# First weights of a second block split during the last expert pair, and a choice of experts by small look-ups: a two-block transformer on one core

## The chip, the core and the metric

The kernel runs on one core of a Trainium2 chip. A core has five engines that run side by side, each with its own queue of instructions, issued in order: TensorE (PE: matrix products; its weight loads are shown as PEld), VectorE (DVE), ScalarE (ACT), GpSimd (POOL) and SyncE (SP), which here mostly issues the DMA loads of the weights. The metric is device time in microseconds (us) from start to end of the program. Three runs of the kernel before took 1753.63, 1758.73 and 1759.56 us; the median is 1758.73 us.

## The reference

Two transformer blocks follow each other on 256 tokens of width 1024, all in float32.

```python
def first_block(x, ...):
    h = x + mixed @ w_out            # stick-breaking attention and spatial gating
    h = h + hierarchical_moe(rmsnorm(h), ...)   # 4 groups x 8 experts, top 2 of a group
    return rmsnorm(h, final_norm_g)

def second_block(x, mem, ...):
    u = rms_norm(h, norm_mix)
    qa, ka, va, qb, kvb, gb, gate_a, gate_b = split(u @ w_in)   # differential and sparse attention
    h = h + merged @ w_out
    h = h + memory_cross_attention(...)
    h = h + peer_ffn(rms_norm(h, norm_ffn), ...)
    return rms_norm(h, norm_final)

def peer_ffn(u, w_q, sub_keys, u_tab, v_tab):     # 16384 experts, tables of 16384 x 1024
    s = einsum(q(u), sub_keys)                    # 8 heads x 2 halves x 128 keys for each token
    top_s, top_i = top_k(s, 16)                   # 16 of each half
    best_s, best_j = top_k(all 16 x 16 sums, 16)  # 16 pairs for each head
    expert = take_along_axis(cand_i, best_j)      # row index * 128 + column index
    g = softmax(best_s)
    out = sum_k g[k] * gelu(u . u_tab[expert[k]]) * v_tab[expert[k]]
```

## The kernel before

Float32 products are made of three products of a narrower form: each weight tile is split into a high part (a copy on ScalarE, L145) and a low part (weight minus high part, on VectorE or GpSimd, L146), and `mm3` (L153 to L155) adds high x high, high x low and low x high. Three buffers each hold high and low parts (`n_hi`, `n_lo`), so a split can start when the half tile three places before it has been used.

The first block ends with `moe`: 32 experts in 16 pairs, p = 0 to 15. A pair takes gate and up products (L777), a silu, transposes, a down product into two accumulators (L805), whose results ScalarE copies out (high part, L813) and VectorE subtracts (low part, L814), and a product by a one-hot matrix that brings the rows back to the tokens; VectorE adds these to X (L716). After `moe` come a rarely needed overflow branch and `phase_c`, the second block. `split_first` (L864 to L871) splits the first quarter of the second block's `w_in` ahead of `phase_c`: high parts L869 on ScalarE, low parts L870 on GpSimd. `phase_c` flips X (eight pairs of transposes L216, with the high part by L217 on ScalarE and the low part by L221 on VectorE; their instructions are kept in the list `flips`), then takes the products of X by the first two quarters, and scales X by its norm.

The expert layer of the second block takes all 16384 rows of U as 64 tiles of two halves (a half is one split of 128x1024 and 24 matmuls), while the choice runs beside it: top-k steps on VectorE (L1423 to L1447), candidates' positions (L1458 to L1469), the softmax (L1474 to L1481, with Exp on ScalarE, L1477), the transposes of its weights on TensorE (L1485), and the look-ups of the chosen indices. A look-up takes, for each of 256 choices a token, the entry at a position 0 to 15 of a list of 16: L1499 compares a position with 0 to 15 (128x2048), L1502 multiplies by the list, L1505 sums 16 by 16; L1507 transposes. There are four of them (two halves of the tokens, row and column). Then one-hot matrices (L1516, L1519) and products L1526 spread the weights over the experts; `N_POOL` says for how many U tiles GpSimd makes the low parts (L1562: `gp=i < N_POOL`).

The order in which instructions stand in each engine's queue comes from a scheduler that simulates a timeline on its own costs; `after(a, b)` forces a behind b. Loads of weights stand in SP's queue in the order of `queue`, each waiting for its buffer (L122).

## Time and profile before

| what | value |
|---|---|
| median of three runs | 1758.73 us |
| profiled execution, its own time | 1757.5 us |
| its span, first to last instruction | 1755.8 us |
| mean granted TensorE clock | 0.989 |
| TensorE busy | 1687.8 us, 96% |
| VectorE busy | 981.4 us, 56% |
| ScalarE busy | 680.9 us, 39% |
| GpSimd busy | 304.9 us, 17% |

The profile is of one execution. Busy time is the time in which an engine has an instruction running; a share over the whole span averages over stages with different limits, so the rows below are taken from single stretches. In a timeline row the first number is the start in us from the span's start, the second how long the instruction (or the group of `xN` equal ones) ran; what stands in brackets is how long the engine had been idle before it and which engine's instruction it had waited for. [...]

### The profile page before, as it was taken

Reading aid. Unit: us, or ns where it says so; the run is one execution under the profiler, and the core shown is the slowest. Engines: PE = TensorE matmul, PEld = TensorE weight load, DVE = VectorE, ACT = ScalarE, POOL = GpSimd, SP = SyncE. Lnnn points to the kernel's source line nnn. Section 1 sums busy time; section 2 is a strip of 40 time slices with the busy share of each in tenths; the row PEclk is TensorE's granted clock in tenths of the full one; section 3 lists DMA queues with packets and bytes.
Section 4 is the critical chain, followed back from the end, with each engine's and each line's share of the span. In section 5 each row is a group of like instructions: output and inputs, shape, how many; then the busy total and the mean of one; then the engine's idle time right before and its main releaser. Section 6 shows DMA issues by size and latency. Waiting matters only on the chain. (4 is left out here: it accounts for less than half of the span.)

```text
span 1755.8 us, 27472 instructions
## 1 busy us (share of the span) xinstructions
PE 1687.8 (96%) x11096; PEld 1330.7 (76%) x11096; DVE 981.4 (56%) x2010; ACT 680.9 (39%) x1148; POOL 304.9 (17%) x176
## 2 busy tenths in 40 slices
PE   8999999999999989999999799999999999999998
PEld 7984454444444369889899799999999978888886
DVE  5462231122222165685658989999999844444444
ACT  6551121111111145455454435444444444444444
POOL 4320000000000033223457400000000022222221
PEclk9998999999999999999999899999999999999999
DMA  9537999899999985533044343444444455565553
GB/s 380 218 112 325 366 407 382 340 398 412 421 420 421 421 333 217 202 112 121 25 145 145 121 168 127 163 168 146 153 161 145 168 192 192 192 228 192 192 193 120
DMA packets 69251, 410.02 MB, mean 234 GB/s; under 512 B 9217, under 2 KB 9857, under 8 KB 28545
## 3 DMA queue, kind: packets, MB, share of 16 engines
q1 hardware_dynamic: 67840, 406.64, 61.4%
q8 instruction: 88, 1.44, 0.3%
q10 hardware_dynamic: 1280, 1.59, 0.2%
q14 instruction: 43, 0.34, 0.1%
HBM read 406.11 MB, written 2.10 MB: 232 GB/s over the span
## 5 line engine op out<-in xcount | busy, mean ns | idle before, releaser
L145 ACT ACTIVATE hi<-w 128x1024 fp32r<-128x1024 f32 x368 | 388.9, 1059 | 506.3 <-PE oa L155 180.6
L146 DVE TENSOR_TENSOR lo<-w,hi 128x1024 fp32r<-128x1024 f32 x260 | 326.9, 1259 | 223.3 <-ACT hi L145 223.1
L146 POOL TENSOR_TENSOR lo<-w,hi 128x1024 fp32r<-128x1024 f32 x108 | 266.9, 2473 | 1011.7 <-ACT hi L145 947.0
L155 PE MATMUL acc<-act,lo 128*128 128x256 f32 x928 | 268.4, 289 | 6.0 <-DVE lo L146 6.0
L153 PE MATMUL acc<-act,hi 128*128 128x256 f32 x928 | 267.7, 289 | 4.0 <-ACT hi L145 2.8
L154 PE MATMUL acc<-act,hi 128*128 128x256 f32 x928 | 265.4, 286 | 0.0
L777 PE MATMUL acc<-w,act 128*64 128x512 f32 x1016 | 246.1, 596 | 4.7 <-DMA w<-w_up 3.5
L154 PE MATMUL acc<-lo,act 128*128 128x256 f32 (+1 forms) x592 | 196.6, 333 | 3.4 <-DVE lo L146 1.6
L155 PE MATMUL acc<-hi,act 128*128 128x256 f32 (+1 forms) x592 | 195.3, 332 | 0.2 <-DVE act L1286 0.2
L155 PEld LDWEIGHTS acc<-act,lo 128*128 128x128 f32 x928 | 179.6, 194 | 10.2 <-DVE lo L146 7.6
L153 PEld LDWEIGHTS acc<-act,hi 128*128 128x128 f32 x928 | 179.6, 194 | 9.4 <-ACT hi L145 5.5
L777 PEld LDWEIGHTS acc<-w,act 128*64 128x64 f32 x1016 | 80.4, 137 | 139.3 <-issue 126.4
L153 PE MATMUL acc<-hi,act 128*128 128x256 f32 (+1 forms) x592 | 177.3, 334 | 3.6 <-ACT hi L145 1.6
L154 PEld LDWEIGHTS acc<-act,hi 128*128 128x128 f32 x928 | 179.6, 194 | 1.2 <-issue 1.2
L153 PE MATMUL oa<-act,hi 128*128 128x256 f32 x528 | 151.7, 287 | 4.0 <-ACT hi L145 3.9
L155 PE MATMUL oa<-act,lo 128*128 128x256 f32 x528 | 152.5, 289 | 0.0
L154 PE MATMUL oa<-act,hi 128*128 128x256 f32 x528 | 150.6, 285 | 0.0
L1519 DVE SCALAR_TENSOR_TENSOR oha<-cols,iT,g 128x384 bf16<-128x384 bf16 x256 | 142.0, 609 | 0.0
L153 PEld LDWEIGHTS acc<-hi,act 128*128 128x128 f32 x592 | 113.4, 192 | 16.7 <-ACT hi L145 3.6
L154 PEld LDWEIGHTS acc<-lo,act 128*128 128x128 f32 x592 | 113.4, 192 | 16.3 <-DVE lo L146 3.3
L805 PE MATMUL oa<-w,mo_h 128*64 128x512 f32 x480 | 125.0, 599 | 0.0
L155 PEld LDWEIGHTS acc<-hi,act 128*128 128x128 f32 x592 | 113.1, 192 | 10.4 <-DVE act L1286 0.4
(423 smaller groups left out, 2523.3 us busy)
## 6 DMA issues: line engine op xcount, KB each, us to landing
w<-w_gate SPq DMA_DIRECT2D x64, 1024.0 KB, 10.7
w<-peer_u SPq DMA_DIRECT2D x64, 1024.0 KB, 4.9
w<-peer_v SPq DMA_DIRECT2D x64, 1024.0 KB, 4.9
w<-w_up SPq DMA_DIRECT2D x63, 1024.0 KB, 12.2
w<-w_down SPq DMA_DIRECT2D x60, 1024.0 KB, 10.6
w<-w_in SPq DMA_DIRECT2D x28, 1024.0 KB, 9.0
w<-w_out SPq DMA_DIRECT2D x8, 1024.0 KB, 16.0
w<-peer_wq SPq DMA_DIRECT2D x8, 1024.0 KB, 4.8
```

The source lines that it names most:

```text
L145: self.last_hi = nc.scalar.activation(hi, src, AF.Copy)
L146: r = (nc.gpsimd if gp else nc.vector).tensor_tensor(lo, src, _f(hi), op=ALU.subtract)
L153: first = mm(ps, lhsT=a[0], rhs=b[0], start=start, stop=False)
L154: mm(ps, lhsT=a[0], rhs=b[1], start=False, stop=False)
L155: return first, mm(ps, lhsT=a[1], rhs=b[0], start=False, stop=stop)
L777: mm = nc.tensor.matmul(ps[nm][e * 64:(e + 1) * 64, :], lhsT=xe[kh][:, k, s0:s0 + CAP], rhs=w[e][:, k, :], start=(kh + k == 0), stop=(kh * ...
L805: nc.tensor.matmul(y[hf][e * 64:(e + 1) * 64, :], lhsT=hT[:, kh * 2 + k, e * 64:(e + 1) * 64], rhs=w[e][k][:, hf * 512:(hf + 1) * 512], st ...
L1519: V.scalar_tensor_tensor(ab[:, t], cols[:, None, :].to_broadcast([128, 3, 128]), iT[:, t0 + t:t0 + t + 1], g3[:, :, t0 + t:t0 + t + 1].to_ ...
```

## The change

1. `N_POOL` falls from 7 to 3: the low parts of U tiles 3 to 6 (eight halves) are made on VectorE instead of GpSimd.
2. The look-ups of the choice: for row and column, 16 instructions `scalar_tensor_tensor` (position == s, times entry s of the list) of 128x256 write 16 layers, and adds of 2048, 1024, 512 and 256 columns sum these. They take both halves of the tokens together, and work in the scores' buffer (`sk`). The transposes of the choice are forced behind the last matmul of U that was issued before them in the program (`last_u`).
3. The first two quarters of `w_in` of the second block are queued at the start of `moe`, behind its own weights, and `split_first` is called within the last pair (p = 15). Its low parts are made on VectorE, and the last evacuations of that pair (`yh`, `yl`) are forced behind it (`split_end`).
4. In `phase_c` the splits of the second quarter, low parts on VectorE, are forced behind flips 4 and 5, the squares of X behind flip 7, and both multiplies of X by the norm's gain stand on VectorE behind the last flip's low part.

```diff
@@ -37,7 +37,7 @@
 
-N_POOL = 7
+N_POOL = 3
 
@@ -171,7 +171,7 @@
 
-    def sumsq(self, rows, junk=None):
+    def sumsq(self, rows, junk=None, after=None):
 
@@ -182,7 +182,9 @@
                 out = junk[:, j, :]
-            self.nc.scalar.activation(out, r, AF.Square, accum_out=ss[:, j:j + 1])
+            sq = self.nc.scalar.activation(out, r, AF.Square, accum_out=ss[:, j:j + 1])
+            if after:
+                self.after(sq, after)
         return ss
@@ -216,9 +218,9 @@
         if g is None:
-            nc.vector.tensor_tensor(lo, pt, _f(hi), op=ALU.subtract)
+            self.flip_lo = nc.vector.tensor_tensor(lo, pt, _f(hi), op=ALU.subtract)
         else:
-            nc.vector.scalar_tensor_tensor(lo, pt, g, _f(hi), op0=ALU.mult, op1=ALU.subtract)
+            self.flip_lo = nc.vector.scalar_tensor_tensor(lo, pt, g, _f(hi), op0=ALU.mult, op1=ALU.subtract)
         return r
@@ -691,13 +693,17 @@
 
-    def moe(self):
+    def moe(self, go_on=True):
         nc, I, X = self.nc, self.I, self.X
...
                 self.queue(I["w_cross_kv_2"][p - M0 - 1])
+        self.wc = self.weights_c()
+        if go_on:
+            for w in self.wc[:2]:
+                self.queue(w, pool="sp")
         self.gains_c()
@@ -791,6 +797,9 @@
                     back_to(*late, 1, tr)
+                if p == 15 and go_on:
+                    first = self.ahead.pop(-2)[0]
+                    self.split_first(first)
                 hT = ht.rearrange("p (k s) -> p k s", k=4)
@@ -810,8 +819,11 @@
                     sl = slice(hf * 512, (hf + 1) * 512)
-                    nc.scalar.activation(yh[:, sl], y[hf], AF.Copy)
-                    nc.vector.tensor_tensor(yl[:, sl], y[hf], _f(yh[:, sl]), op=ALU.subtract)
+                    ev = [nc.scalar.activation(yh[:, sl], y[hf], AF.Copy),
+                          nc.vector.tensor_tensor(yl[:, sl], y[hf], _f(yh[:, sl]), op=ALU.subtract)]
+                    if p == 15 and go_on:
+                        for a, b in zip(ev, self.split_end):
+                            self.after(a, b)
                 late = yh, yl, PT, pr
@@ -861,13 +873,14 @@
 
-    def split_first(self):
-
-        w = self.next_w().rearrange("p (k n c) -> p n k c", k=8, n=2)
+    def split_first(self, w=None):
+
+        w = (self.next_w() if w is None else w).rearrange("p (k n c) -> p n k c", k=8, n=2)
         hi, lo = [self.act(F32R).rearrange("p (n k c) -> p n k c", n=2, k=8) for _ in range(2)]
         for n in range(2):
-            self.nc.scalar.activation(hi[:, n], w[:, n], AF.Copy)
-            self.nc.gpsimd.tensor_tensor(lo[:, n], w[:, n], _f(hi[:, n]), op=ALU.subtract)
+            hi_ = self.nc.scalar.activation(hi[:, n], w[:, n], AF.Copy)
+            lo_ = self.nc.vector.tensor_tensor(lo[:, n], w[:, n], _f(hi[:, n]), op=ALU.subtract)
+        self.split_end = hi_, lo_
         self.w_first = [(hi[:, n], lo[:, n]) for n in range(2)]
@@ -909,11 +922,16 @@
         xT = self.xpair(X, self.g2)
-        ahead = [self.dense_T(w, xT, ps=self.oacc) for w in (self.w_first, self.next_w())]
+        ahead = [self.dense_T(self.w_first, xT, ps=self.oacc)]
+        w, second = self.next_w(), []
+        for n in range(2):
+            second.append(self.part_T(w, n, gp=False))
+            self.after(self.last_hi, self.flips[4 + n])
+        ahead.append(self.dense_T(second, xT, ps=self.oacc))
         xs = act().rearrange("p (j d) -> p j d", j=2)
-        r1 = self.rstd(self.sumsq(lambda j: X[:, j, :], xs), 2, D, "x")
+        r1 = self.rstd(self.sumsq(lambda j: X[:, j, :], xs, self.flips[7]), 2, D, "x")
         for j in range(2):
-            (V, nc.gpsimd)[j].tensor_tensor(xs[:, j, :], X[:, j, :], fg, op=ALU.mult)
+            self.after(V.tensor_tensor(xs[:, j, :], X[:, j, :], fg, op=ALU.mult), self.flip_lo)
         ss = self.sumsq(lambda j: xs[:, j, :], "hi")
@@ -1482,31 +1500,34 @@
                 js = slice(j * 128, (j + 1) * 128)
-                nc.tensor.transpose(pt[:, js], wt[:, js], self.ident)
+                self.after(nc.tensor.transpose(pt[:, js], wt[:, js], self.ident), self.last_u)
             nc.scalar.activation(g3[:, 0], pt, AF.Copy)
...
             yield
-            eq = xe[:, 1024:].bitcast(BF16)
-            eq3 = eq.rearrange("p (n s) -> p n s", s=16)
-            eq4 = eq.rearrange("p (h k s) -> p h k s", h=8, k=16)
-            for j in range(2):
-                js = slice(j * 128, (j + 1) * 128)
-                xj = xb[:, j].rearrange("p (h c) a -> p h c a", c=2)
-                for c, pos in enumerate((rf, cf)):
-                    V.tensor_tensor(eq3, pos[:, js, None].to_broadcast([128, 128, 16]),
-                                    self.iota[:, None, :16].to_broadcast([128, 128, 16]), op=ALU.is_equal)
-                    yield
-                    V.tensor_tensor(eq4, eq4, xj[:, :, c, None, :].to_broadcast([128, 8, 16, 16]), op=ALU.mult)
-                    yield
-                    hf = u[:, c * 128:(c + 1) * 128]
-                    V.tensor_reduce(hf, eq3, axis=AX.X, op=ALU.add)
-                    pt = self.wk()
-                    nc.tensor.transpose(pt[:, :128], hf, self.ident)
-                    nc.scalar.activation(tabs[c][:, js], pt[:, :128], AF.Copy)
-                    yield
+
+            eq = sk.rearrange("p n c -> p (n c)").bitcast(BF16).rearrange("p (s n) -> p s n", s=16)
+            eq4 = eq.rearrange("p s (n k) -> p s n k", k=16)
+            x4 = xb.rearrange("p j (h c) a -> p (j h) c a", c=2)
+            for c, pos in enumerate((rf, cf)):
+                pos3 = pos.rearrange("p (n k) -> p n k", k=16)
+                for s in range(16):
+                    V.scalar_tensor_tensor(eq4[:, s], pos3, float(s), x4[:, :, c, s:s + 1].to_broadcast([128, 16, 16]),
+                                           op0=ALU.is_equal, op1=ALU.mult)
+                    if s % 4 == 3:
+                        yield
+                for n in (8, 4, 2):
+                    V.tensor_tensor(eq[:, :n], eq[:, :n], eq[:, n:2 * n], op=ALU.add)
+                V.tensor_tensor(u, eq[:, 0], eq[:, 1], op=ALU.add)
+                yield
+                pt = self.wk()[:, :256]
+                for j in range(2):
+                    js = slice(j * 128, (j + 1) * 128)
+                    self.after(nc.tensor.transpose(pt[:, js], u[:, js], self.ident), self.last_u)
+                nc.scalar.activation(tabs[c], pt, AF.Copy)
+                yield
 
@@ -1559,8 +1580,8 @@
                 for k in range(8):
-                    self.mm3(ps[:, e, :], (hi[:, k, :], lo[:, k, :]), (xT[0][:, k, :], xT[1][:, k, :]),
-                             k == 0, k == 7)
+                    self.last_u = self.mm3(ps[:, e, :], (hi[:, k, :], lo[:, k, :]), (xT[0][:, k, :], xT[1][:, k, :]),
+                                           k == 0, k == 7)[1]
             n = self.t_done
@@ -1671,12 +1692,8 @@
                         K.cp = K.tp
-                        K.moe()
+                        K.moe("c" in parts)
                         K.n_am = 0
-                        if "c" in parts:
-                            K.wc = K.weights_c()
-                            K.queue(*K.wc[:2])
-                            K.split_first()
                         K.overflow()
```

The next pieces are the order of instructions on an engine, before and after. First ScalarE's queue around Exp: `hi` is a high part of a U half, `H` a copy of U's results out of an accumulator, `ce` the working tile of the choice, `g_1379` the weights of the choice. Before:

```order
L1570 ACTIVATE H_7529<-acc_8394 128x512
L145 ACTIVATE hi_8603<-w_8392 128x1024
L145 ACTIVATE hi_8663<-w_8488 128x1024
L1570 ACTIVATE H_7529<-oa_8490 128x512
L1477 ACT_TABLE_LOAD
L1477 ACTIVATE ce_7418<-ce_7418,rs_7515 128x128 x2
L145 ACTIVATE hi_8691<-w_8488 128x1024
L145 ACTIVATE hi_8729<-w_8572 128x1024
```
Exp stands ahead of the high parts of the second half of tile `w_8488` and of all of `w_8572`.

ScalarE's queue around Exp after:

```order
L1591 ACTIVATE H_7529<-oa_8490 128x512
L145 ACTIVATE hi_8694<-w_8488 128x1024
L145 ACTIVATE hi_8738<-w_8572 128x1024
L1591 ACTIVATE H_7529<-acc_8574 128x512
L145 ACTIVATE hi_8766<-w_8572 128x1024
L145 ACTIVATE hi_8806<-w_8663 128x1024
L1591 ACTIVATE H_7529<-oa_8665 128x512
L1495 ACT_TABLE_LOAD
L1495 ACTIVATE ce_7418<-ce_7418,rs_7515 128x128 x2
L145 ACTIVATE hi_8834<-w_8663 128x1024
L145 ACTIVATE hi_8878<-w_8735 128x1024
```
Exp (L1477, now L1495) stands behind two more copies of `H` and four more high parts of U than before.

Then VectorE's queue at the first look-ups; `lo` is a low part of a U half. Before (compare, multiply and sum are L1499, L1502, L1505):

```order
L1499 TENSOR_TENSOR ce_7418<-ce_7418,iota 128x2048
L1487 TENSOR_TENSOR ce_7418<-wk_8651,g_1379_7532 128x256
L1502 TENSOR_TENSOR ce_7418<-ce_7418 128x2048
L1489 TENSOR_TENSOR ce_7418<-ce_7418,g_1379_7532 128x256
L1505 TENSOR_REDUCE ce_7418<-ce_7418 128x128
L146 TENSOR_TENSOR lo_8795<-w_8660,hi_8794 128x1024
L1499 TENSOR_TENSOR ce_7418<-ce_7418,iota 128x2048
L146 TENSOR_TENSOR lo_8823<-w_8660,hi_8822 128x1024
```
The first look-up is done in three instructions ahead of the first low split here, and the second begins between two splits.

VectorE's queue at the same place after (look-ups L1517, adds L1522 and L1523; L1505 and L1507 are now subtracts that belong to the weights of the choice):

```order
L146 TENSOR_TENSOR lo_8879<-w_8735,hi_8878 128x1024
L1517 SCALAR_TENSOR_TENSOR ce_7418<-ce_7418 128x256 x6
L1505 TENSOR_TENSOR ce_7418<-wk_8651,g_1379_7532 128x256
L1517 SCALAR_TENSOR_TENSOR ce_7418<-ce_7418 128x256 x10
L146 TENSOR_TENSOR lo_8907<-w_8735,hi_8906 128x1024
L1507 TENSOR_TENSOR ce_7418<-ce_7418,g_1379_7532 128x256
L146 TENSOR_TENSOR lo_8951<-w_8803,hi_8950 128x1024
L1522 TENSOR_TENSOR ce_7418<-ce_7418 128x2048
L146 TENSOR_TENSOR lo_8979<-w_8803,hi_8978 128x1024
L1522 TENSOR_TENSOR ce_7418<-ce_7418 128x1024
L1517 SCALAR_TENSOR_TENSOR ce_7418<-ce_7418 128x256 x8
L146 TENSOR_TENSOR lo_9037<-w_8875,hi_9036 128x1024
```
The sixteen look-ups of the first table stand between two low splits, without one among them; those of the second table stand in groups of two to eight, with low splits between.

Last the end of the last expert pair. ScalarE before, where L813 copies out the pair's results and L869 makes the high parts of the first quarter (`w_4073`) of `w_in`:

```order
L780 ACTIVATE mo_s_4007<-acc_3969 128x512
L791 ACTIVATE mo_h_4023<-wk_4018 128x512
L813 ACTIVATE yh_4033<-oa_4035 128x512
L813 ACTIVATE yh_4033<-oa_4036 128x512
L869 ACTIVATE act_4077<-w_4073 128x1024 x2
```
The split of the first quarter stands behind both evacuations.

ScalarE at the same place after (L822 was L813, L881 was L869):

```order
L786 ACTIVATE mo_s_4011<-acc_3969 128x512
L797 ACTIVATE mo_h_4027<-wk_4022 128x512
L881 ACTIVATE act_4037<-w_3982 128x1024 x2
L822 ACTIVATE yh_4043<-oa_4045 128x512
L822 ACTIVATE yh_4043<-oa_4046 128x512
```
It stands ahead of both now.

VectorE at the end of the last pair after (L882 makes the low parts, L823 was L814, L722 was L716):

```order
L722 TENSOR_TENSOR X<-X,wk_4033 128x512
L882 TENSOR_TENSOR act_4038<-w_3982,act_4037 128x1024 x2
L823 TENSOR_TENSOR yl_4044<-oa_4045,yh_4043 128x512
L823 TENSOR_TENSOR yl_4044<-oa_4046,yh_4043 128x512
L722 TENSOR_TENSOR X<-X,wk_4067 128x512
L722 TENSOR_TENSOR X<-X,wk_4071 128x512
L722 TENSOR_TENSOR X<-X,wk_4075 128x512
L722 TENSOR_TENSOR X<-X,wk_4079 128x512
```
The two splits of the first quarter, on ScalarE and on VectorE, stand ahead of the last pair's evacuations, and with these ahead of the last four adds to X.

## Rows read from the trace of the kernel before

**Rows 1.** Waits of TensorE over the whole span: us in total, times, longest.

```profile
PE wk L1485 <- DVE ce L1481: 10.0, 1, 10.0
```

**Rows 2.** Stretches: length, busy PE PEld DVE ACT POOL, PEclk, DMA share, GB/s.

```profile
984.10:994.07 9.97, 0.00 (x1) 0.03 (x1) 9.83 (x53) 4.47 (x6) 2.96 (x2) 0.72 0.00 0
994.07:998.74 4.67, 4.67 (x22) 4.67 (x23) 4.63 (x5) 1.44 (x2) 3.38 (x2) 0.50 0.65 225
998.74:1015.81 17.07, 14.21 (x115) 13.59 (x113) 17.04 (x18) 7.55 (x11) 3.20 (x1) 1.00 0.37 124
1015.81:1022.63 6.82, 5.92 (x27) 5.93 (x28) 5.31 (x4) 1.04 (x1) 0.00 (x0) 0.50 0.46 154
```

**Rows 3.** Timeline of ScalarE: start, us, instruction, idle before and releaser.

```profile
989.39 0.69 ACT L1477 ACTIVATE ce<-ce,rs 128x128 f32<-128x128 f32 x2 [9.88 <-DVE ce L1474]
```

**Rows 4.** Timeline of VectorE, end of the choice and first look-ups.

```profile
966.25 2.35 DVE L1469 CAST ce<-ce 128x256 bf16<-128x256 uint32 x1
...
990.82 0.38 DVE L1462 SCALAR_TENSOR_TENSOR ce<-ce 128x256 f32<-128x256 f32 x1
991.12 0.28 DVE L1463 TENSOR_SCALAR ce<-ce 128x256 f32<-128x256 f32 x1
991.33 2.60 DVE L1481 TENSOR_TENSOR ce<-ce,tk_z 128x256 f32<-128x256 f32 x1
993.84 2.61 DVE L1464 TENSOR_TENSOR ce<-ce 128x256 f32<-128x256 f32 x1
...
996.58 0.41 DVE L1465 TENSOR_TENSOR ce<-ce 128x256 f32<-128x256 f32 x1
996.91 0.41 DVE L1467 TENSOR_TENSOR ce<-ce 128x256 f32<-128x256 f32 x1
997.36 2.29 DVE L1499 TENSOR_TENSOR ce<-ce,iota 128x2048 bf16<-128x2048 f32 x1
...
1008.93 1.22 DVE L146 TENSOR_TENSOR lo<-w,hi 128x1024 fp32r<-128x1024 f32 x1
1010.06 4.32 DVE L1519 SCALAR_TENSOR_TENSOR oha<-cols,iT,g 128x384 bf16<-128x384 bf16 x8
1014.30 1.22 DVE L1502 TENSOR_TENSOR ce<-ce 128x2048 bf16<-128x2048 bf16 x1
```

**Rows 5.** Timeline of GpSimd, low splits of U tiles.

```profile
966.01 2.44 POOL L146 TENSOR_TENSOR lo<-w,hi 128x1024 fp32r<-128x1024 f32 x1 [0.43 <-ACT hi L145]
...
991.11 5.05 POOL L146 TENSOR_TENSOR lo<-w,hi 128x1024 fp32r<-128x1024 f32 x2 [10.87 <-ACT hi L145]
```

**Rows 6.** Timeline of TensorE, half 6 of U (tile 3).

```profile
970.50 0.28 PE L153 MATMUL oa<-act,hi 128*128 128x256 f32 x1
...
970.74 0.28 PE L155 MATMUL oa<-act,lo 128*128 128x256 f32 x1
```

**Rows 7.** Timeline of SP, and DMA issues from 607.5 to 611 (KB each, us to landing).

```profile
607.73 2.81 SPq L122 DMA_DIRECT2D w<-w_in  x2
...
w<-w_in SPq DMA_DIRECT2D x2, 1024.0 KB, 19.8
```

**Rows 8.** The hand-over: timelines of ScalarE, VectorE, TensorE, and one stretch.

```profile
629.28 2.00 ACT L869 ACTIVATE act<-w 128x1024 fp32r<-128x1024 f32 x2
...
629.41 0.69 DVE L814 TENSOR_TENSOR yl<-oa,yh 128x512 fp32r<-128x512 f32 x1 [0.58 <-ACT yh L813]
630.02 2.47 DVE L716 TENSOR_TENSOR X<-X,wk 128x512 f32<-128x512 f32 x4
...
642.41 2.27 DVE L970 TENSOR_TENSOR lam<-lam 128x1 f32<-128x1 f32 x1
...
636.64 0.45 PE L216 MATMUL wk<-ident,X 128*128 128x128 f32 x2 [2.17 <-DVE act L221]
...
645.13 0.38 PE L154 MATMUL oa<-act,act 128*128 128x256 f32 x1 [1.29 <-DVE lam L972]
...
636.93:640.34 3.41, 3.41 (x19) 3.41 (x18) 3.41 (x7) 2.26 (x6) 3.31 (x10) 0.50 0.95 229
```

## The prediction

> **What bounds the kernel now.** I read in this order: the list of what TensorE waits for, the stretches around the largest entry, the rows of each engine there, then the rows at the place where the first block hands over to the second. TensorE is busy nearly all the time, so only its gaps and its half-clock stretches can be won. The longest single gap in the list is one of 10.0 us, for the transposes of the choice weights (L1485), which wait for VectorE's L1481 [rows 1]. [...] Together 9.97 + 2.33 + 2.86 + 3.86 = **19.0 us** between 984.10 and 1022.63.
>
> Why it stalled: ScalarE issues in order. Its Exp (L1477) stands ahead of the high-part splits that the next tiles of U need, and it waited 9.88 us for VectorE's L1474, the last step of the choice [rows 3, 4]. So TensorE starved behind an instruction that it needs only much later. VectorE itself was late in part because of GpSimd: while GpSimd does the low-part split of a U tile (rows of about 2.44 us), a VectorE instruction takes as long as the split: CAST L1469 takes 2.35 us beside such a row, L1481 2.60 and L1464 2.61 beside the next pair, and L1465, of L1464's form, 0.41 after it [rows 4, 5].
>
> **The choice stage after the change.** A half tile of U is 24 matmuls; the first and third of half 6 start at 970.50 and 970.74, 0.12 apart, so a half takes 24 x 0.12 = 2.88 us and half n is wanted from 970.50 + 2.88 (n - 6) [rows 6].
>
> Exp. By the order it now stands two tiles later on ScalarE, with four more high-part splits ahead of it, and the transposes are forced behind matmuls of U that stand ahead of them. TensorE reaches them at half 14 and a quarter, about 970.5 + 8.25 x 2.88 = 994.3 plus what it waits. L1474 ends in before where Exp starts, at 989.4. Eight splits at 1.13 us now stand ahead of it, and 6.2 us of lengthening go (both worked out below): 989.4 + 9.0 - 6.2 = 992.2; the choice weights follow, with one more split between, at 995.7, about when TensorE gets to their transposes. Exp and the high part behind it end near 994, and half 15 wants that part at 970.5 + 9 x 2.88 = 996.4 plus the waits so far, 1.4: some 4 us of slack. The 19.0 us go, unless VectorE's new load makes waits of its own.
>
> VectorE's load. From the CAST at 966.25 to the first look-up at 997.36 before spends 31.1 us. Five rows there are lengthened as shown (two CASTs, L1447, L1481, L1464); from 2.60 and 2.61 to 0.41 the last two lose 4.4, the other three 6.2 at about 2.1 each, 10.6 in all. No GpSimd split is left beside them: 20.5. Into it come 11 low splits (halves 6 to 16) at 1.13 us from start to start (1008.93 to 1010.06) [rows 4]: 12.4. The first look-up thus starts near 966.25 + 32.9 = 999.2, some 2 us later than in before, but TensorE no longer waits for it.
> - Half 6: its split stands behind 4.4 us of other work after 966.25, ends near 971.9, and TensorE wants it with its third matmul at 970.74: a wait of 1.2. Half 8, behind the next top-k rows: 0.2.
> - The look-ups: two tables of 16 small scalar_tensor_tensor of 128x256 and four adds each. No row of before has that instruction. Nearest rows: L1462, the same operation and tile size, lasts 0.38 us and the next starts 0.30 after it; L1465 lasts 0.41, 0.33 to the next; L1519, 128x384, takes 4.32 for eight, 0.54 each [rows 4]. Ends: 0.30 and 0.54; I take 0.33, since L1462 is the nearest in form and size. The order puts all 16 of the first table between the splits of halves 16 and 17: 16 x 0.33 + 0.33 for the subtract of the choice's weights among them = 5.6, so split 17 ends near 999.2 + 5.6 + 1.1 = 1005.9, and TensorE wants it at 970.74 + 11 x 2.88 + the 1.4 already waited + 0.3 for transposes = 1004.1: a wait of 1.8.
> - The second table is spread between the splits (2 to 8 look-ups at a time beside steps of 2.88 us) and hides. Behind split 23 stand an add of 128x2048 and eight one-hots: 1.1 + 4.3 + 1.1 for the split, against 2.88 and the lead that VectorE has by then: a wait of about 1.1.
> - The four large adds are bf16 128x2048 like L1502, which took 1.22 us at 1014.30 [rows 4]; I take 1.1 apart. At an upper end of 2.3 (L1499's form, row 997.36) two waits grow by some 3 us in all.
> Waits that come: 1.2 + 0.2 + 1.8 + 1.1 = **4.3**. At 0.54 for a look-up the wait for split 17 alone grows by 16 x 0.21 = 3.4 and the second table uses up its cover: some 11 in all; the other end, 0.30, gives 3.8. The stretch before the second fall of the clock held 2.86 us of idle time in 17; these waits are shorter and, but for the first two, over 20 us apart, so I count no fall. Net of the stage: 19.0 - 4.3 = **14.7**. Fewer, smaller evacuations and the removed 128x2048 compare, multiply and reduce lie on ScalarE and VectorE beside full TensorE work: nothing more.
>
> [...]
>
> **The hand-over.** SP issues the first two w_in loads at 607.73, which land 19.8 us later (median of the two), the first at 627.5 [rows 7]; the order of SP's queue does not change. In before ScalarE evacuates the last expert pair first, VectorE subtracts behind it (0.69 us for each of two) and adds the last rows to X (630.02, ending at 632.49); ScalarE splits w_in from 629.28, in 2.00 us, and GpSimd makes the low parts [rows 8]. In after the two splits stand ahead of the evacuations on ScalarE and, with the low parts, on VectorE. So ScalarE does L881 at 627.55 to 629.55; VectorE the low parts, at 1.22 each as in row 1008.93, to 631.05; the two subtracts follow to 632.35 (0.65 apart) and the four adds to X, 2.47, end at 634.85: X is **2.36 us later**. Queued behind it: the transposes of X, the whole first product. What goes: TensorE's waits of 2.17 and 1.29 us among these transposes and products, since GpSimd's splits no longer stretch VectorE's rows to some 2.3 us there (row 642.41 is a 128x1 multiply of 2.27), and the half-clock stretch of 3.41 us, which loses up to 1.7 [rows 8]. All of it: 2.17 + 1.29 + 1.7 - 2.36 = 2.8; but a longer first wait can bring a half-clock stretch of its own (then 1.1), and the second weight's splits, now forced behind flips 4 and 5, can stand in the way for one VectorE split of 1.13 more (then 0). I take **0.5**; ends -2.4 (the delay is paid and nothing comes back) and +2.8.
>
> **Sum.** Against the profiled execution's own 1757.5 us (span 1755.8 and 1.7 around it): 1757.5 - 14.7 - 0.5 = 1742.3, so **1742 us**. The profile is 1.2 below the median of the runs, 1758.73, and inside their spread of 1753.63 to 1759.56.
>
> **Rivals.**
> A. Look-ups cost a price of 0.41 to 0.54 each, whatever their size. Eight or more VectorE instructions then separate splits that TensorE needs. For: the only long row of this operation, L1519, is 0.54 apart. Against: it is half again as wide. Waits 7 to 11: 1745 to 1749. [...]
> B. The hand-over costs instead of giving, 2.4, and one or two new waits drop the clock for a stretch like the 3.41 us one (1.7 each): 1742.3 + 2.9 + 1.7 to 3.4 = 1747 to 1749. For: 2.86 us of idle time in the choice stage were followed by 6.82 us at half clock [rows 2]. Against: the new waits stand alone.
> C. Exp's wait comes back in part: VectorE, with eight splits more, ends the choice later than 996, and ScalarE again holds a U split. Each microsecond past the 4 of slack is paid: 3 to 8 paid gives 1745 to 1750, and with a half-clock stretch of 1.7 behind it up to 1752; the full old wait of 10 gives 1754. For: the splits and the choice share one engine, in an order made without the lengthened rows. Against: 4 us is more than three splits.
> D. Slower than before: VectorE becomes the bound of the choice stage, because a look-up of 256 elements with a broadcast operand is held up as L970 is (642.41: 2.27 us for one element a row) [rows 8]. Each 0.1 us on a look-up costs up to 3.2. The gain is gone from 0.8 us each (32 x 0.47 = 15.0); at 1.05, 32 x 0.72 = 23 more, the end is 1765. For: VectorE is busy 17.04 of the 17.07 us after the stall already [rows 2]. Against: L970 lies beside a GpSimd split, and these leave the stage.
> E. The change does less than it says, since the top-k itself bounds: covered by C; nothing else in the stage waits for GpSimd.
>
> **How the numbers follow.** My forecast 0.59, with its own range of 1738 to 1746 (look-ups from 0.30 to 0.45, the hand-over from -2.4 to 2.8); A 0.14, B 0.12, C 0.06 (half of it within 0.3%), D 0.09 (0.05 slower, 0.04 within). E has no share of its own. The range for 8 in 10 runs from 1736 (no waits for halves 6 and 24, the hand-over's 2.8, and half of the wait for split 17) to 1752 (the far ends of A, B and C). A measurement of this kernel tells about 0.3%, 5.3 us, from no change: faster means under 1753.4. That holds in the forecast, A, B and half of C: 0.88; within 0.07; slower 0.05.
>
> **What would show it.** In the profile after: no wait near 10 us at the transposes of the choice, and no half-clock stretch between 984 and 1023; Exp's wait on ScalarE under 2 us; TensorE waits of 1 to 2 us for VectorE's low split at halves 6, 17 and 24, and no others above 0.5 in the stage; look-ups 0.30 to 0.35 us apart; CAST and L1464's form at 0.3 to 0.4 us. At the hand-over: X complete about 2.4 us later against the last expert product, and the waits among the transposes of X gone. Wrong I would be if look-ups stand 0.45 us or more apart, if ScalarE's Exp waits over 4 us, or if the stretch from the last expert pair to the first product of the second block grows by over 3 us.

## The result and the profile after

Five runs of the changed kernel took 1744.90 to 1749.37 us, median 1747.55; five of the kernel before beside them 1753.63 to 1759.56, median 1756.34. The ratio is **0.9949, 95% interval 0.9938 to 0.9961**: about 9 us faster. A second set of five gave 1746.55 against 1756.40, ratio 0.9945 (0.9933 to 0.9958). The forecast was 1742 with a range of 1736 to 1752, 15.2 us below the profiled execution: the direction is right and most of the places, the size is 1.7 times too large.

The profiled execution of after took 1745.04 us (span 1743.3), 12.5 less than that of before. The page's first line of busy times, of after:

```profile
PE 1684.5 (97%) x11096; PEld 1326.2 (76%) x11096; DVE 970.4 (56%) x2050; ACT 680.7 (39%) x1146; POOL 273.6 (16%) x164
```

Span less busy time of TensorE is 1743.3 - 1684.5 = 58.8 us, in before 1755.8 - 1687.8 = 68.0. So 9.2 of the 12.5 us are waits that went; the other 3.3 are TensorE's own busy time: in all its stretches at half clock (PEclk, the share of its full clock that TensorE was granted, at 0.50) together it was busy for 28.6 us in before and for 18.9 in after.

Of the choice, first ScalarE and VectorE in the timeline of after (columns as in [rows 3, 4]; L1495 is Exp, L1499 was L1481, L1517 the look-ups):

```profile
990.39 1.28 ACT L1495 ACT_TABLE_LOAD   x1
991.69 0.70 ACT L1495 ACTIVATE ce<-ce,rs 128x128 f32<-128x128 f32 x2
```
```profile
965.74 0.28 DVE L1487 CAST ce<-ce 128x256 bf16<-128x256 uint32 x1
...
993.95 0.42 DVE L1499 TENSOR_TENSOR ce<-ce,tk_z 128x256 f32<-128x256 f32 x1
...
998.30 2.09 DVE L1517 SCALAR_TENSOR_TENSOR ce<-ce 128x256 bf16<-128x256 f32 x6
...
1000.65 3.43 DVE L1517 SCALAR_TENSOR_TENSOR ce<-ce 128x256 bf16<-128x256 f32 x10
1004.00 1.21 DVE L146 TENSOR_TENSOR lo<-w,hi 128x1024 fp32r<-128x1024 f32 x1
```

Exp has no bracket: it waits for nothing, where it waited 9.88 us [rows 3]. The choice itself ends no earlier: its last step, L1492 (L1474 before), ends at 991.64 instead of 989.36. The CAST takes 0.28 us instead of 2.35 and L1499 0.42 instead of 2.60 [rows 4]: no split of GpSimd lies beside them. Ten look-ups last 3.43 and the next instruction starts 3.35 after the first, 0.335 each.

TensorE's waits in the stage, in the timeline of after (the number in brackets is the wait):

```profile
971.44 0.39 PE L155 MATMUL oa<-act,lo 128*128 128x256 f32 x1 [1.04 <-DVE lo L146]
...
1005.27 0.39 PE L155 MATMUL acc<-act,lo 128*128 128x256 f32 x1 [1.27 <-DVE lo L146]
...
1026.45 0.38 PE L153 MATMUL oa<-act,hi 128*128 128x256 f32 x1 [0.79 <-ACT hi L145]
...
1040.09 0.28 PE L1547 MATMUL wk<-oha,ohb 128*128 128x128 bf16 x2 [0.47 <-DVE oha L1540]
...
1042.78 0.39 PE L153 MATMUL acc<-act,hi 128*128 128x256 f32 x1 [0.78 <-ACT H L1591]
```

Three smaller ones for the one-hots (0.18, 0.20, 0.20) stand between the last two. Together 4.9 us. In before the waits of this stage are the 9.97 [rows 2] and these three (L1507 transposes a look-up's result):

```profile
1005.74 0.33 PE L1507 MATMUL wk<-ident,ce 128*128 128x128 f32 x1 [0.93 <-DVE ce L1505]
...
1014.16 0.39 PE L153 MATMUL oa<-act,hi 128*128 128x256 f32 x1 [0.79 <-ACT hi L145]
...
1016.71 0.58 PE L155 MATMUL acc<-act,lo 128*128 128x256 f32 x1 [2.04 <-DVE lo L146]
```

Together 9.97 + 0.93 + 0.79 + 2.04 = 13.7. The wait at the transposes is gone. But half clock came back in another place, right behind the last of these waits (stretch of after; columns as in [rows 2]):

```profile
1043.47:1046.89 3.42, 3.42 (x19) 3.33 (x18) 3.42 (x8) 0.58 (x1) 0.00 (x0) 0.50 0.03 5
```

The hand-over in the timelines of after (L882 makes the low parts, L722 adds to X, L645 is the overflow branch, L195 scales the identity for a later product):

```profile
627.20 2.00 ACT L881 ACTIVATE act<-w 128x1024 fp32r<-128x1024 f32 x2 [6.47 <-SPq L645]
...
628.29 2.36 DVE L882 TENSOR_TENSOR act<-w,act 128x1024 fp32r<-128x1024 f32 x2 [6.46 <-ACT act L881]
...
631.84 2.48 DVE L722 TENSOR_TENSOR X<-X,wk 128x512 f32<-128x512 f32 x4
...
649.52 2.46 DVE L195 TENSOR_SCALAR diag<-ident,rs 128x128 f32<-128x128 f32 x2
...
649.32 2.38 POOL L146 TENSOR_TENSOR lo<-w,hi 128x1024 fp32r<-128x1024 f32 x1 [0.82 <-PE oa L155]
...
629.74 0.49 PE L718 MATMUL wk<-yh,mo_PT 128*128 128x512 f32 x1 [1.32 <-ACT yh L822]
631.30 0.50 PE L721 MATMUL wk<-yl,mo_PT 128*128 128x512 f32 x1 [1.07 <-DVE yl L823]
634.52 1.06 PE L218 MATMUL wk<-ident,X 128*128 128x128 f32 x8 [1.31 <-DVEq L645]
```

X ends at 631.84 + 2.48 = 634.32, 1.83 us later than in before [rows 8]; counted from the start of a wait for w_up ahead of it (613.85 in before, 613.51 in after) it is 2.17. The eight pairs of transposes then run nearly without a wait, but TensorE waits 1.32 + 1.07 + 1.31 ahead of them, and 1.42 later for L195, which takes 2.46 beside a GpSimd split that now falls on it (two instructions, 0.48 together, in before). In before TensorE waited 1.57 ahead of the first transposes, then the 2.17 and the 1.29 of [rows 8].

For the experiments two lengths are read from each profile. The stretch of U runs from the start of one wait to the start of another, which every kernel has (in after):

```profile
896.31 0.39 PE L153 MATMUL acc<-raw,hi 128*128 128x256 f32 x1 [1.56 <-ACT raw L219]
...
1349.82 0.39 PE L155 MATMUL acc<-act,lo 128*128 128x256 f32 x1 [1.02 <-DVE lo L146]
```

That is (1349.82 - 1.02) - (896.31 - 1.56) = 454.0 us, against 466.0 in before: 12.0 of the 12.5. The hand-over, from the 1.3 us wait for w_up to a wait of 0.70 us for L1047, takes 79.56 against 79.65; where that wait is absent, a 0.81 us wait behind it is taken (95.9 and 96.0).

### The profile page after: what moved, and what is told of

Read it like the earlier page. It is cut to its first block, busy times and chain, and to the rows that moved or that the text cites. A ratio compares the mean times of both kernels' runs of the same rounds, so it can differ in the third digit from the quotient of the medians.

```text
span 1743.3 us, 27495 instructions
## 1 busy us (share of the span) xinstructions
PE 1684.5 (97%) x11096; PEld 1326.2 (76%) x11096; DVE 970.4 (56%) x2050; ACT 680.7 (39%) x1146; POOL 273.6 (16%) x164
## 4 chain that ended last, share of the span: by engine, by line
PE 55%; DVE 4%; issue 1%; ACT 1%; POOL 1%; POOLq 0%; DVEq 0%; ACTq 0%
PE acc L155 10%; PE acc L153 10%; PE acc L154 10%; PE oa L153 6%; PE oa L155 6%; PE oa L154 6%; PE wk L1547 2%; DVE lo L146 1%; PE wk L1203 1%; ACT hi L145 0%; POOL lo L146 0%; PE wk L1568 0%; PE oa L1237 0%; PE wk L1126 0%; PE wk L1224 0%
## 5 line engine op out<-in xcount | busy, mean ns | idle before, releaser
L146 DVE TENSOR_TENSOR lo<-w,hi 128x1024 fp32r<-128x1024 f32 x269 | 335.0, 1247 | 221.6 <-ACT hi L145 221.5
L146 POOL TENSOR_TENSOR lo<-w,hi 128x1024 fp32r<-128x1024 f32 x99 | 242.1, 2446 | 1022.8 <-ACT hi L145 928.7
L814 PE MATMUL oa<-w,mo_h 128*64 128x512 f32 x480 | 125.0, 599 | 0.0
```

What stands on the lines that cost most here:

```text
L146: r = (nc.gpsimd if gp else nc.vector).tensor_tensor(lo, src, _f(hi), op=ALU.subtract)
L814: nc.tensor.matmul(y[hf][e * 64:(e + 1) * 64, :], lhsT=hT[:, kh * 2 + k, e * 64:(e + 1) * 64], rhs=w[e][k][:, hf * 512:(hf + 1) * 512], st ...
```

## Experiments

All with their profile; the ratios are to the kernel before on the same chip. Idle is the span less TensorE's busy time in the profile (before 68.0, after 58.8). Medians of before were 1754.33, 1756.40 and 1756.26 us beside the three groups e, f and g.

| run | what | median us | ratio (95%) | stretch of U | idle |
|---|---|---|---|---|---|
| e1 | before, Exp (and the transposes) later | 1747.74 | 0.9968 (0.9954 to 0.9981) | 457.8 | 61.2 |
| e2 | after, seven tiles on GpSimd | 1754.10 | 0.9993 (0.9984 to 1.0002) | 460.9 | 64.9 |
| e3 | before, three tiles on GpSimd | 1750.47 | 0.9969 (0.9958 to 0.9981) | 459.5 | 61.8 |
| e4 | before, new hand-over | 1755.08 | 1.0002 (0.9991 to 1.0013) | 462.8 | 65.6 |
| f1 | after again | 1746.55 | 0.9945 (0.9933 to 0.9958) | 455.4 | 58.8 |
| f2 | after, look-ups twice | 1758.19 | 1.0015 (1.0007 to 1.0024) | 466.7 | 67.1 |
| f3 | after, evacuations first | 1744.11 | 0.9928 (0.9914 to 0.9943) | 455.6 | 55.9 |
| f4 | f3, two splits earlier | 1746.53 | 0.9943 (0.9930 to 0.9956) | 457.9 | 58.3 |
| g1 | after, Exp in its old place | 1750.54 | 0.9970 (0.9959 to 0.9981) | 459.0 | 61.1 |
| g2 | before again | 1755.41 (one run) | | 464.9 | 67.6 |
| g3 | f3, second low part later | 1741.40 | 0.9925 (0.9912 to 0.9938) | 452.9 | 56.7 |
| g4 | g3, split of half 17 earlier | 1741.70 | 0.9918 (0.9905 to 0.9930) | 455.0 | 55.5 |

The gain by the ratio lies within 3.5 us of the idle time that went, in each run that has a ratio.

### e1: Exp's place

```diff
-                nc.scalar.activation(wt[:, js], wt[:, js], AF.Exp, ...)
+                self.exps.append(nc.scalar.activation(wt[:, js], wt[:, js], AF.Exp, ...))
...
+                if i == 5:
+                    for z in self.exps:
+                        self.after(z, h_)      # h_: copy of tile 5's results
```

> The kernel before with one thing added: Exp of the choice is forced behind the copy of U tile 5's results, so that on ScalarE it stands where it stands in the changed kernel, and the transposes of the choice weights follow at half 14 instead of 10.7. GpSimd still makes the low parts of seven tiles and the look-ups are the old ones. Theory of the place (the wait was that Exp stood ahead of U's splits): the 9.97 us wait goes, some 2 to 4 us of waits for VectorE's low splits beside the 128x2048 look-ups stay; the stretch of U from 895 to the 1.02 us wait at 1361 (466.0 us before, 454.0 after the change) takes 453 to 457, the time is 9 to 13 below before. Rival of the load (VectorE is late because GpSimd holds it up and the look-ups are long, the place only follows): 2 or more waits of 3 us and more come instead, the stretch takes 461 or more.

The place alone gives 5.6 us by the ratio, though GpSimd keeps its seven tiles and the look-ups are the old ones. It is two places: with Exp on ScalarE the transposes of the choice weights move on TensorE, behind some 84 more matmuls of U. No run moves one of the two alone. TensorE's waits for the choice and the look-ups in its timeline:

```profile
993.19 0.39 PE L155 MATMUL oa<-act,lo 128*128 128x256 f32 x1 [2.90 <-DVE lo L146]
...
1039.05 0.33 PE L1507 MATMUL wk<-ident,ce 128*128 128x128 f32 x1 [1.61 <-DVE ce L1505]
```

The wait of 9.97 is gone and 2.90 is the largest. The profile's stretch, 457.8, is 0.8 over the upper end of what the theory of the place gave; the time gained, 5.6 for 9 to 13, is about half of it.

### e2, e3, e4: the parts of the change

```diff
# e2, on after
-N_POOL = 3
+N_POOL = 7
# e3, on before
-N_POOL = 7
+N_POOL = 3
# e4: after with N_POOL = 7 and before's choice() (look-ups, transposes unforced)
```

> The changed kernel with seven U tiles on GpSimd again. Exp then stands again two tiles earlier on ScalarE, as in before; the small look-ups, their forced transposes and the hand-over stay changed. Theory of the place: the wait of about 10 us at the transposes is back, with half clock behind it; only the later waits (0.93, 0.79 and 2.04 us in before) shrink with the shorter look-ups: the stretch of U takes 460 to 464, the time is 1 to 5 below before. Rival of the look-ups (they are what freed VectorE): the wait is under 5 us and the stretch takes 457 or less.

> The kernel before with three instead of seven U tiles on GpSimd and nothing else. By the order Exp moves two tiles later on ScalarE. Theory of the place: the stretch of U takes 454 to 458, since the old look-ups cost VectorE some 8 us more than the new ones, of which a part shows as waits; the time is 8 to 12 below before. Rival of the look-ups: the eight splits more on VectorE without shorter look-ups give back what Exp gains, the stretch takes 461 or more.

> The kernel before with the hand-over alone changed: first weights split within the last pair, low parts on VectorE, the forced orders in the second block; seven tiles on GpSimd and the old look-ups. My theory: X comes 2.3 us later and the waits among its transposes go, which about cancels: from the 1.3 us wait for w_up at 613.8 to the 0.70 us wait at 693.5 (79.65 us before, 79.56 after) it takes 78.5 to 80.5, and the time agrees with before within 2 us. Rival: the hand-over gains by itself and loses it to a half-clock stretch only in some executions: the time is 2 to 4 below before. Second rival: the choice needs it (its DMAs stand differently): the stretch of U changes by over 1 us, from 466.0.

With seven tiles on GpSimd (e2) Exp stands early, the wait is back with 7.71 us, and the new look-ups bring 1.2 us, within the interval of none. Three tiles alone (e3) bring 5.4, the same as e1, which has Exp and the transposes in the same place and seven tiles on GpSimd: what three tiles buy there is the place. Now the old look-ups are what is late next:

```profile
1042.67 0.48 PE L1507 MATMUL wk<-ident,ce 128*128 128x128 f32 x1 [6.05 <-DVE ce L1505]
```

So the new look-ups, with their forced transposes and the new hand-over, are worth about 4 us (0.9945 to 0.9949 against 0.9969, intervals that just touch), but only where the wait for the choice is out of the way. Both theories had e3 wrong in part: 459.5 lies between their two ranges. The hand-over alone (e4) changes no time, as I reckoned, but not in the way I reckoned. It takes 82.7 us, over my 78.5 to 80.5 and 3.1 more than in before, with two stretches at half clock in it (at 630.97 and 654.87). Its stretch of U, 462.8 instead of 466.0, hit the second rival's sign and gives 3.2 back. The instructions there stand in the order of before, and what differs is the clock: one fall behind the wait instead of two, and one ahead, at 900.62, which brings TensorE later to a wait that is then 7.75 instead of 9.97.

```profile
995.40 0.66 PE L1503 MATMUL wk<-ident,ce 128*128 128x128 f32 x2 [7.75 <-DVE ce L1499]
```
```profile
992.78:999.61 6.83, 4.21 (x20) 4.24 (x21) 6.80 (x6) 3.88 (x5) 5.55 (x3) 0.50 0.42 154
```

The first row is the wait, the second the only stretch at half clock behind it. In before these were 10.2 and 6.8 us.

### g1: Exp back in its old place

```diff
+                if 2 * i + e == 11:
+                    for z in self.exps:
+                        self.after(self.last_hi, z)
```

> The changed kernel (three tiles on GpSimd, the new look-ups, the new hand-over) with one thing put back: the high part of half 11 is forced behind Exp, as it stands in the kernel before. Theory of the place: ScalarE holds the U splits again until VectorE has ended the choice, which with five low splits ahead of it is about 988; TensorE wants half 11 at 986 and then its transposes: waits of 5 to 8 us together around 986, half clock behind them, the stretch of U takes 459 to 464 (454.0 and 455.4 in two executions of the changed kernel), the time is 4 to 9 above the changed kernel's. Rival of the load: with VectorE free of GpSimd's locks the choice is early enough for the old place; waits under 2 us, the time rises by under 2.

ScalarE and TensorE in its timeline:

```profile
990.85 0.69 ACT L1495 ACTIVATE ce<-ce,rs 128x128 f32<-128x128 f32 x2 [3.20 <-DVE ce L1492]
```
```profile
992.54 0.58 PE L153 MATMUL oa<-act,hi 128*128 128x256 f32 x1 [3.94 <-ACT hi L145]
```

Exp waits again, but 3.20 instead of 9.88, and TensorE 3.94 for the high part behind it, under the 5 to 8 that I gave; the transposes follow without a wait. The ratio is 0.9970, 4.4 us worse than after by the ratios: at the lower end of what the theory of the place gave, and over the rival's 2. Still, 5.3 us of the gain are there with Exp early.

The rival's reason, an earlier choice, is not what the rows show: Exp's operand was ready at 990.82, in before at 989.36. Counted from the 1.56 us wait at the start of the stretch, TensorE came to the wait 4.0 us later than in before: behind a wait of 1.04 at half 6, ten more matmuls, and, in this execution, a fall of the clock at 899. And the wait ended 2.1 earlier: L1499 takes 0.42 here, the same step in before, L1481, 2.60 beside the GpSimd splits that Exp had held up [rows 4, 5], and the transposes no longer stand ahead of half 11. So neither theory stands alone, and the two gains overlap (5.6 + 5.3 against 9).

### f2: what a look-up costs

```diff
+                    for _ in range(2):
                     V.scalar_tensor_tensor(eq4[:, s], pos3, float(s), ...)
```

> The changed kernel with each of the 32 look-ups issued twice. My theory: a look-up takes 0.335 us of VectorE and those of the first table lie bare between the splits of halves 16 and 17: the wait at half 17 grows from 1.27 by 16 x 0.335 = 5.4 to 6.6 us; the second table is covered for the most part (0 to 3 us more): the stretch of U takes 459.5 to 463 (454.0 with single look-ups), the time is 5 to 9 above the changed kernel. Rival of the cover (VectorE's lead takes both tables): the wait at half 17 stays under 3 us, the time rises by under 2. Rival of the fixed cost: a repeated look-up costs 0.42 or more, and 11 us or more come.

```profile
1000.00 4.79 DVE L1518 SCALAR_TENSOR_TENSOR ce<-ce 128x256 bf16<-128x256 f32 x14
```
```profile
1009.33 0.58 PE L155 MATMUL acc<-act,lo 128*128 128x256 f32 x1 [5.99 <-DVE lo L146]
...
1026.26 0.39 PE L155 MATMUL acc<-act,lo 128*128 128x256 f32 x1 [2.23 <-DVE lo L146]
```

The price stays 0.33 to 0.34 (4.79 for 14), so the fixed cost of 0.42 is out (0.415 us is the mean length of a single look-up in after, but there too the next one starts 0.335 behind it), though the time that this rival gave came, and the wait at half 17 is near what I gave (5.99 for 6.6). The time rose by 11.6, not 5 to 9: span less busy grew from 58.8 to 67.1, 8.3 us for 32 x 0.335 = 10.7 us of look-ups added, as the second table showed too (2.23 at 1026, 0.52 ahead of it, 1.92 instead of 0.78 at the one-hots). Three stretches at half clock followed (1006.95, 1027.43 and 1054.73). So VectorE has little cover in this stage.

### f1 and g2: the same kernels again

> The changed kernel once more, on the same chip as the three below. Theory of the clock (the waits are the same in each execution, the half-clock stretches are not, and the 19.0 us I read from one execution held 6 us of them): the waits over 0.4 us in the stretch of U are the same to 0.2 us (1.04, 1.27, 0.79, 0.78 at the one-hots), the half-clock stretches lie elsewhere in part, and the ratio to before is 0.994 to 0.997. Rival of the profile (what the pair of profiles showed, 12.5 us, is the true gain): ratio 0.992 to 0.993.

> The kernel before once more, for a second look. Theory of the clock: the same waits to 0.2 us (9.97, 0.93, 0.79, 2.04), but other half-clock stretches; the stretch of U takes 461 to 467, and less than 466.0 where the second fall (6.8 us at 1015.8) is not there. Rival: the stretches follow the waits strictly, and 10.2 and 6.8 us at half clock stand again behind 988 and 1015.

The waits repeat: 1.04, 1.27, 0.79, 0.47 and 0.78 in f1; 9.94, 1.38, 0.79 and 2.04 in g2, where 1.38 for 0.93 is more than the 0.2 that I gave. Span less busy is 1743.7 - 1684.9 = 58.8 in f1, the same as in after, and 1753.7 - 1686.1 = 67.6 in g2. The half clock repeats in part. Stretches of g2, then of f1:

```profile
986.52:996.76 10.24, 3.69 (x18) 3.73 (x19) 10.07 (x26) 5.91 (x8) 5.36 (x3) 0.50 0.29 100
1017.24:1020.65 3.41, 3.41 (x18) 3.41 (x17) 3.04 (x3) 1.06 (x1) 0.00 (x0) 0.50 0.86 274
```
```profile
896.13:899.55 3.42, 3.42 (x19) 3.42 (x17) 2.04 (x6) 1.63 (x4) 1.23 (x1) 0.50 1.05 386
1042.91:1046.32 3.41, 2.97 (x14) 2.98 (x15) 3.41 (x8) 1.16 (x3) 0.00 (x0) 0.50 0.02 5
```

In before the clock falls again behind the same two waits (the rival's point), the second time for 3.4 instead of 6.8 us; in after it falls behind the one-hots' waits again, and in f1 once more at 896, where the first profile has none. The ratio 0.9945 is as the theory of the clock had it.

### f3, f4, g3, g4: on from there

```diff
# f3, on after
-                    if p == 15 and go_on:
-                        for a, b in zip(ev, self.split_end):
-                            self.after(a, b)
...
-            return lambda: self.dense_R(self.next_w(), xT, evac)
+            return lambda: self.dense_R(self.next_w(), xT, evac, gp=None if c else False)
# f4, on f3: look-ups 8 to 15 of the first table behind the low split of half 17,
#     first maxima of heads 1 to 7 behind that of half 6
# g3, on f3: the low part of the first weight's second half
+        self.after(self.second_low(), self.flip_los[1])
# g4, on g3: look-ups 8 to 15 behind the low split of half 17
```

> The changed kernel with another hand-over: the last pair's evacuations are not forced behind the split of the first weights (by the order they then stand ahead of it again), and the low part of the third weight's halves is made on VectorE instead of GpSimd. My theory: the waits of 1.32 and 1.07 us for yh and yl go, that for VectorE's branch grows by about 1 because both low parts stand ahead of it, and the 1.42 us wait for the scaled identity (two rows lengthened to 2.46 beside a GpSimd split) goes: the hand-over from the 1.3 us wait for w_up to the 0.70 us wait at 693 takes 76.5 to 78.5 us instead of 79.6, the time is 1 to 3 below the changed kernel. Rival: what is won in waits is lost again behind it, since the second weights' split is late next: 79 to 80.5 us, no change.

> The hand-over of the run before, and in the choice eight look-ups of the first table forced behind the split of half 17 and most of the top-k's first maxima behind the split of half 6. My theory: the wait at half 17 falls from 1.27 to 0.6 or less and that at half 6 from 1.04 to 0.5 to 1, nothing new over 0.5 comes: the stretch of U takes 452.5 to 454 with a half-clock stretch, a time of 2 to 5 below the changed kernel with the hand-over's gain. Rival: the held look-ups push the second table and the one-hots back, and the waits at halves 22 to 28 grow by as much: the stretch stays at 454 or more.

> The changed kernel with the evacuations first, the third weight's low parts on VectorE, and the second low part of the first weight moved behind the second flip, so that only one stands ahead of VectorE's branch. My theory: TensorE's wait of 3.85 us for VectorE's branch (of the run with the evacuations first) falls by 1.1 to 1.2, nothing new comes behind it, the waits in all are 46.5 to 47.5 us instead of 48.0, the time is 0.5 to 2 below that run. Rival: the transposes of X wait for ScalarE and VectorE in turn, and the 1.2 us come back among the flips.

> The same with eight look-ups of the first table forced behind the low split of half 17, and nothing held behind half 6. My theory: the wait of 1.27 at half 17 goes, that of 1.04 at half 6 stays, and at the one-hots 0.5 to 1.3 come back, as in the run with both splits earlier (0.97 and 1.35 instead of 0.47 and four small ones): no gain over the run before it by more than 1. Rival: the one-hots were late there because of the half-6 split alone, and 1.3 to 2 us are won.

TensorE's wait ahead of the transposes of X in f3, then in g3:

```profile
633.95 1.94 PE L218 MATMUL wk<-ident,X 128*128 128x128 f32 x8 [3.85 <-DVEq L645]
```
```profile
632.60 1.94 PE L219 MATMUL wk<-ident,X 128*128 128x128 f32 x8 [2.71 <-DVEq L647]
```

f3 trades 1.32 + 1.07 + 1.31 for 3.85 at one place, no gain, but the wait of 1.42 behind GpSimd's split falls to 0.24; its median is 2.4 us below that of f1 beside it, with intervals that overlap. Its 0.70 us wait is gone, so the forecast length can't be read; to the 0.81 us wait it is 95.1 (after: 95.9; f1: 98.8, of which 1.6 are a longer wait for w_up). g3 takes the branch's wait down by 1.14, as forecast, and that length is 93.3 in g3 and 93.6 in g4 against 95.1 and 95.2 in f3 and f4. But span less busy is 56.7 us against 55.9 in f3: the waits in all did not fall, as forecast, but rose by 0.8, outside the hand-over, and the ratios of the two agree (0.9925 and 0.9928). Its median, 2.7 below that of f3, is no sure gain: in its profile the clock fell once between 150 and 1734 us, in that of f3 four times. f4 lost what it should win: the wait at half 6 is gone, but the held maxima now stand ahead of the low split of half 7, for which TensorE waits 2.50 (the first row below),

```profile
976.33 0.39 PE L156 MATMUL oa<-act,lo 128*128 128x256 f32 x1 [2.50 <-DVE lo L146]
...
1042.56 0.34 PE L1549 MATMUL wk<-oha,ohb 128*128 128x128 bf16 x3 [1.35 <-DVE oha L1542]
```

and the wait of half 17 came back at the one-hots (second row), as the rival said. g4, without the part on half 6, shows the same 1.36 there and agrees with g3. Both are 13 to 14 us faster than the kernel before, and g4's interval lies below that of the changed kernel; between the two nothing is decided.

## Why the prediction held, and where its size was off

**Exp.** Right that it goes. The wait of 9.97 is not there, Exp waits for nothing, and the high part behind it ends at 993.3, some 4 us before half 15 starts (997.6): the slack that was given. But ScalarE was only part of the reason. In before the first of these two high parts is that of half 11:

```profile
989.99 1.99 ACT L145 ACTIVATE hi<-w 128x1024 fp32r<-128x1024 f32 x2
```

It was ready at 991.03. TensorE stood until 994.07 at the transposes in its own queue, for L1481, which ended at 993.93, lengthened beside the two GpSimd splits that these high parts had let go [rows 4, 5]. That the place lets go of U is shown by e1 and g1: e1 moves Exp and the transposes, g1 shows ScalarE's hold alone, 3.94. That the place is the only reason is not shown: 5.3 us come with Exp early.

**VectorE's load.** Right in the price and the places, and by chance right to half a microsecond in the sum. Look-ups stand 0.335 apart (0.33 taken); waits of 1.04, 1.27 and 0.79 came where 1.2, 1.8 and 1.1 were given (the third for ScalarE's high part, not for the low one), and the 0.2 at half 8 did not: 3.1 for 4.3. What was not given are the waits at the first one-hots, 0.47 + 0.18 + 0.20 + 0.20 + 0.78 = 1.8: the second table ends so late that the one-hots follow on it. In all 4.9 against 4.3.

**The clock.** This step failed: "Together 9.97 + 2.33 + 2.86 + 3.86 = 19.0 us", and "so I count no fall". Of the 19.0, 13.7 are waits, and the other 5.3 are the price of half clock in one execution: 4.67 and 5.92 us of work at 0.50 [rows 2], of which I counted half as lost, 2.33 and 2.96. No run shows that half: the matmuls of U stand 0.213 us apart at 0.50 in before (18 steps from 994.74 to 998.58) and 0.12 at 1.00 [rows 6], so 0.44 of the time was lost there, about 4.6 us by this estimate. The waits of the stage came again to 0.5 us in the second execution of each kernel (g2, f1). Of the price, the fall behind the longest wait came each time (4.67 and 3.69 us worked at half clock in before and g2, 4.10 and 4.21 in e2 and e4); the next one did not: 3.4 instead of 6.8 us in g2, none in e4 with the same instructions. And after pays for its own: 3.4 us at 1043 in both profiles, another at 896 in one of them. In the pair of profiles 3.3 us of busy time went, in the second pair (g2, f1) 1.2. The waits alone, 68.0 - 58.8 = 9.2, are near what the timed runs show, 8.8 to 9.9 by the medians; their intervals, 6.8 to 11.8 us by the ratios, leave room for some 2 us of half clock beside them. With the clock's 5.3 left out, the forecast's own terms give 13.7 - 4.3 + 0.5 = 9.9.

**The hand-over.** The 0.1 us of the first pair of profiles is near the 0.5 forecast, but by the luck of the draw. The old hand-over takes 79.65 to 79.67 us in the four profiles that have it (before, g2, e1, e3), with 3.4 to 6.1 us of work at half clock in it: so the 1.7 that I counted for that stretch was not there to win. The new one takes 79.6 in after, where the clock did not fall, and 80.9 to 82.7 in the five others that have it (f1, e2, f2, g1, e4; f1 and e2 less their longer wait for w_up), where it fell once or twice. So it costs 1 to 3 us more often than not. X came 2.17 later, counted from the wait for w_up, where 2.36 was given. The waits of 1.57, 2.17 and 1.29 went, and four of 1.32, 1.07, 1.31 and 1.42 came, the last from a GpSimd split moved onto a pair of VectorE instructions, which I had not looked for.

**The rivals.** A and D: the price of a look-up, 0.335 us, is that of its neighbours of the same size (L1462 0.30, L1465 0.33 [rows 4]), and stays so in f2 (0.33 to 0.34). An element costs more in the small form: 32 look-ups of 256 elements take 11.2 us by the groups of after, 1.37 ns an element, and the twelve compares, multiplies and sums of 2048 elements 25.0 by those of before, 1.02 ns an element. The small form wins, 11.2 + 5.4 with its eight adds, because it passes over fewer elements, 15872 instead of 24576. f2 shows that VectorE can become the bound, as D has it: doubled, the look-ups make the kernel slower than before (1.0015). But D's reason is not shown: a look-up there lasts 0.429 us at the mean, and L970's 2.27 lay beside a multiply on GpSimd (L916, 2.42 us from 642.25), not beside a split. C did not happen. Much of B is there: the hand-over costs in five profiles of six, and the clock falls at other places.

## What to carry to other kernels

Read a stall's cost as two terms: the waits, which came again here to 0.5 us in a second execution, and the half clock behind them, which is in part a draw; count only the first as a gain unless several executions show the second. An instruction that waits on an in-order queue costs what stands behind it, so look for its place in the queue before its speed, and on every queue that it holds up: here later places on two queues were worth 5.6 us with nothing made faster. And when work moves off one engine, see what the remaining work of that engine now falls beside: here a GpSimd split of 2.38 us fell beside L195's pair, which took 2.46 us instead of 0.48.

## What the runs showed of the hardware that I had not expected

Between 895 and 901 us the clock fell in seven of the executions profiled (e2, e4, f1, f3, f4, g1, g4), all with the new hand-over, and in none of the others, although the 1.56 us wait ahead of it is the same in all; after, f2 and g3 have the new hand-over and no fall there. A fall thus depends on more than the wait before it, and what decides it stays open. Of g2's stretch of 10.24 us at half clock only 3.69 were busy; in the rest TensorE was idle. Over all the profiles TensorE's busy time grows from 1681.9 us with 13.8 us worked at half clock (g3) to 1689.0 with 29.6 (e4), 0.45 us for each; and in the old hand-over even that cost no length, where TensorE then waits less (the 1.29 us wait is 0.34 in g2).
